# Hybrid decoder layer on one core: the four plain down-projection blocks row by row, a last half row in two 256-column pieces, 16 filler products instead of 24, and a new table of instruction places

## The chip, the cores and the metric

The kernel runs on one core of a Trainium2 chip. A time is the device time of one execution in microseconds (us). Before the change three runs took 617.90, 619.43 and 617.29 us, so the median is 617.9 us. A profiled execution has a time of its own and, a little shorter, a span: the time from its first to its last instruction. All positions in the trace are counted from the start of the span.

The engines are named as in the profile: PE is the matrix engine (PEld its weight loads), DVE the vector engine, ACT the scalar engine, POOL the general engine, and SP the engine that starts nearly all transfers.

## The reference: what is computed

One decoder layer for 512 tokens and a model width of 1024, in float32:

```
h = modulate(rms_norm(x, pre_norm_mix), sh1, sc1)
y = hybrid_mixer(h, ...)          # RG-LRU group and sparse-attention group, each RMS-normalised, then w_out
x = x + (1 + g1) * rms_norm(y, post_norm_mix)
h = modulate(rms_norm(x, pre_norm_mlp), sh2, sc2)
y = square(relu(h @ w_ff1)) @ w_ff2        # w_ff1: 1024 x 4096, w_ff2: 4096 x 1024
x = x + (1 + g2) * rms_norm(y, post_norm_mlp)
```

The six vectors sh, sc and g come from one product of silu(c) with a 1024 x 6144 matrix. The change is about the last product (the "down-projection" with w_ff2) and the last line, about the opening of the program, and about the order of everything between.

## The kernel before

**Precision.** Every large product is made from three products of a faster number format: an operand is split into a high part (hi, made by a copy on ACT or DVE) and a low part (lo, made by a subtraction on DVE or POOL), and `mm3` (line 908) multiplies hi by hi, hi by lo and lo by hi into the same PSUM bank. So each block of weights costs ACT, DVE and POOL work before PE may use it, and this splitting runs ahead of PE through four buffers of parts and four of raw weights (class `Weights`, line 469).

**Stages.** The opening loads x and the first weights, normalises x (`norm_x`), forms the first shift and scale by 16 narrow products with silu(c) (tile `tp`, from `sil` and `p` in the trace) and transposes x on PE. Before the transposes can start, PE runs filler products (`WARM`, lines 38 and 877): each multiplies a corner of x with the identity into a bank of the coming stage that is overwritten later; in the trace they are `s<-r,ident`, and one filler shows as two records. Then come the input projection ("first wave", matmuls `<-h,hi_a`), the recurrent group and the attention mixed with each other (roughly 50 to 260 us), the output projection, the up-projection with w_ff1 (280 to 450 us), and the down-projection (450 to 607 us).

**Down-projection.** w_ff2 has 32 blocks of 128 rows. 28 of them go through a scheme that saves products by adding blocks first: 14 pairs in a first pass (weights `D0` to `D13`), then a second pass (`e0` to `e13`). The last four blocks (28 to 31, weights `s28` to `s31`) are plain. Output is 4 rows of 128 tokens by 2 halves of 512 columns, eight half rows in eight PSUM banks; `rows` (lines 1774 and 1775) lists them. Before the change, block 28 is multiplied into all eight half rows first, and then the last `G_LAST` = 3 blocks half row by half row (line 1776). When a half row is done, DVE adds it to what the first pass left (`ob`), ACT squares it with a sum (`junk<-r`), and DVE or POOL multiply it by the row `g2row`; when both halves of a row are done, `finish` (line 1736) adds the two sums on DVE (`stat`), POOL takes the power -1/2 (`stat<-stat,nhalf`), DVE combines each half with x (SCALAR_TENSOR_TENSOR), and SP stores it (`out<-r`).

**Order.** The order written in the code isn't the order on the engines. Every operation is recorded as a node, and `flush` (line 274) issues the nodes in the order of a table of numbers, `PLAN`, one number per node; each engine then runs its own nodes in that order and waits where an input isn't there. `PLACE` says, for each operation that two or three engines could do, which one does it. Operations carry the line of a helper: 334 matmul, 337 transpose, 344 ACT, 376 DVE and POOL, 418 transfers started by SP.

## Time and profile before

| | before |
|---|---|
| three runs, us | 617.90, 619.43, 617.29 (median 617.9) |
| the profiled execution's time, us | 618.04 |
| its span, us | 616.3 |
| PE busy, share of the span | 590.4 us, 96% |
| DVE busy | 554.3 us, 90% |
| ACT busy | 406.1 us, 66% |
| POOL busy | 167.4 us, 27% |
| mean clock granted to PE | 0.993 |

PE is idle for 25.9 us of the span: until the first x has come, for some 12 us in short waits inside, and for 9 us at the end. A busy PE is not a PE at its peak: matmuls overlap, and a matmul's length in the trace includes its way through the array. The distance from one start to the next says more: it is about 0.227 us for 512 columns and 0.12 us for 256 columns in the dense stretches. Durations at one engine that follow each other overlap in the same way, by about 0.1 us.

### The profile page before, as it was taken

The numbers are of one execution on the slowest core, as the hardware profiler recorded it, in microseconds if no ns is written. First come the engines' busy times: TensorE is split into PE (matmuls) and PEld (weight loads), VectorE is DVE, ScalarE is ACT, GpSimd is POOL, SyncE is SP. The second block draws the span as 40 slices with busy tenths as digits, with TensorE's granted clock in tenths as the row PEclk, the third lists the DMA queues.
The fourth block names the chain that finished last, engine by engine and source line by source line (L and its number), as shares of the span: only waits on it lengthen the run. The fifth ranks groups of instructions, "written<-read, shape, count | busy, mean of one in ns | idle before, by whom it ended". The sixth has DMA issues, their size and how long they took to land.

```text
span 616.3 us, 10061 instructions
## 1 busy us (share of the span) xinstructions
PE 590.4 (96%) x3504; PEld 514.7 (84%) x3504; DVE 554.3 (90%) x1152; ACT 406.1 (66%) x824; POOL 167.4 (27%) x189
## 2 busy tenths in 40 slices
PE   6999999999889999999999999999998999999994
PEld 6888989977768898879999999998867888888883
DVE  5897999989989998889999989999899999999827
ACT  6546317999999899896856555656466666654312
POOL 5104010325335448541033233213000000211143
PEclk9999999999989999999999999999999999999998
DMA  8996994240305311022334323335423445443303
GB/s 350 369 351 264 336 367 171 102 151 22 129 11 204 137 36 35 0 87 69 137 137 138 110 97 121 104 103 188 137 87 115 149 130 163 162 138 109 130 0 137
DMA packets 26842, 89.10 MB, mean 145 GB/s; under 512 B 2980, under 2 KB 3236, under 8 KB 26792
## 3 DMA queue, kind: packets, MB, share of 16 engines
q1 hardware_dynamic: 26648, 88.40, 40.4%
q8 instruction: 27, 0.44, 0.3%
q14 instruction: 23, 0.19, 0.1%
q10 hardware_dynamic: 144, 0.07, 0.1%
HBM read 86.36 MB, written 2.10 MB: 144 GB/s over the span
## 4 chain that ended last, share of the span: by engine, by line
PE 76%; DVE 13%; ACT 7%; issue 2%; DMA 1%; POOL 0%; DVEq 0%; ACTq 0%
PE f L334 26%; PE s L334 18%; PE pv L334 16%; PE tp L334 12%; PE tp L337 4%; DVE fT L376 3%; DVE fl L376 1%; ACT p L344 1%; DVE lo_B L376 1%; DVE lo_C L376 1%; DVE lo_D L376 1%; ACT h L344 1%; ACT r L344 1%; ACT L344 1%; ACT junk L344 1%
## 5 line engine op out<-in xcount | busy, mean ns | idle before, releaser
L334 PE MATMUL f<-hi_o,h 128*128 128x512 f32 x128 | 46.1, 413 | 1.3 <-ACT h L344 1.1
L344 ACT ACTIVATE p<-p,mx 128x32 f32<-128x32 f32 (+4 forms) x96 | 45.1, 472 | 1.4 <-DVE mx L376 1.4
L344 ACT ACTIVATE hi_B<-raw_A 128x512 fp32r<-128x512 f32 x35 | 22.1, 631 | 28.5 <-DVE raw_A L376 21.0
L334 PE MATMUL pv<-pt,V 128*128 128x256 f32 x160 | 37.9, 308 | 2.3 <-ACT pt L344 2.1
L334 PE MATMUL s<-K,Q 128*128 128x288 f32 (+4 forms) x128 | 36.6, 333 | 0.8 <-DVE mx L376 0.8
L337 PE MATMUL tp<-ident,p 128*128 128x128 f32 x192 | 37.0, 273 | 0.4 <-DVE pt L376 0.4
L376 DVE TENSOR_TENSOR pt<-tp,pt 128x512 fp32r<-128x512 f32 (+1 forms) x56 | 33.9, 609 | 3.3 <-ACT pt L344 1.9
L344 ACT ACTIVATE fT<-fT 128x512 f32<-128x512 f32 x50 | 30.6, 623 | 2.7 <-DVE fT L376 2.2
L334 PEld LDWEIGHTS pv<-pt,V 128*128 128x128 f32 x160 | 27.0, 191 | 6.3 <-ACT pt L344 2.5
L376 POOL TENSOR_SCALAR p<-p,den 128x32 f32<-128x32 f32 (+4 forms) x33 | 28.9, 886 | 6.5 <-DVE den L376 2.9
L344 ACT ACTIVATE junk<-r 128x1024 bf16<-128x1024 f32 (+1 forms) x20 | 17.8, 888 | 16.8 <-DVE r L376 16.8
L337 PEld LDWEIGHTS tp<-ident,p 128*128 128x128 f32 x192 | 24.5, 140 | 4.8 <-issue 1.1
L376 DVE CUSTOM_DVE_ANT_0 p<-p,silb 128x1024 f32<-128x1024 f32 x23 | 27.9, 1221 | 0.1
L334 PEld LDWEIGHTS f<-hi_o,h 128*128 128x128 f32 x128 | 23.2, 189 | 5.4 <-ACT h L344 1.4
L334 PE MATMUL f<-lo_o,h 128*128 128x512 f32 x64 | 25.9, 410 | 0.0
L334 PEld LDWEIGHTS s<-K,Q 128*128 128x128 f32 x128 | 22.4, 188 | 3.4 <-issue 0.7
L344 ACT ACTIVATE hi_D<-raw_D 128x1024 fp32r<-128x1024 f32 x14 | 14.8, 1058 | 14.3 <-DVE raw_D L376 5.1
L334 PE MATMUL tp<-r,hi_B 128*128 128x256 f32 x96 | 23.0, 285 | 0.1
L344 ACT ACTIVATE pt<-tp 128x512 fp32r<-128x512 f32 (+1 forms) x38 | 19.8, 534 | 4.5 <-PE tp L337 3.5
L344 ACT ACTIVATE hi_e<-raw_e 128x1024 fp32r<-128x1024 f32 x13 | 13.8, 1062 | 13.5 <-PE s L334 4.3
L334 PE MATMUL pv<-r,hi_B 128*128 128x256 f32 x96 | 22.5, 284 | 0.0
L376 DVE TENSOR_TENSOR lo_B<-raw_A,hi_B 128x512 fp32r<-128x512 f32 x32 | 22.0, 686 | 0.5 <-ACT hi_B L344 0.2
(424 smaller groups left out, 2312.0 us busy)
## 6 DMA issues: line engine op xcount, KB each, us to landing
p<-in_ada_a SPq DMA_DIRECT2D x16, 512.0 KB, 7.4
ar<-in_ada_r SPq DMA_DIRECT2D x16, 512.0 KB, 4.1
p<-in_ada_t SPq DMA_DIRECT2D x16, 512.0 KB, 5.5
raw_d<-in_wd SPq DMA_DIRECT2D x14, 512.0 KB, 3.2
raw_e<-in_wd SPq DMA_DIRECT2D x14, 512.0 KB, 3.4
raw_A<-in_wf SPq DMA_DIRECT2D x12, 512.0 KB, 3.3
raw_B<-in_wf SPq DMA_DIRECT2D x12, 512.0 KB, 3.7
r<-in_x SPq DMA_DIRECT2D x8, 512.0 KB, 4.7
```

Of the source, the lines that this page charges most:

```text
L334: lambda: self.nc.tensor.matmul(out, lhs, rhs, start=start, stop=stop))
L337: self.issue("pe", 0.109, [out], [src], lambda: self.nc.tensor.transpose(out, src, ident))
L344: return "act", cost, lambda: self.nc.scalar.activation(out, src, func, scale=scale, bias=bias, **kw), func
L376: return eng, cost, lambda: fn(out, *args, **kw), None
```

## The change

`WARM` goes from 24 to 16. `G_LAST` goes from 3 to 4: no block is multiplied into all half rows first any more, and all four plain blocks are taken half row by half row. The last half row in the list (row 3, columns 0 to 511) is no longer accumulated on top of the second pass: that pass's bank is closed and added to `ob` early, and the four blocks go into two fresh banks as two pieces of 256 columns, each with its own sum of squares; `finish` for that row adds three sums instead of two and stores three parts instead of two. `PLAN` and `PLACE` are new tables throughout.

```diff
-G_LAST = 3
+G_LAST = 4
-WARM = 24
+WARM = 16
 PLAN = (
-    '###(#8#A#&#M#E#1#5#7#;#C#T#Y#`#b#k#=#B#P#p#z#$#%#)#-#+#,#.#2#J#/#w#[#0#6#9#D#I#h#l#n#t#|#~$$$-$2$4$8'
...
 def times(what, way, fs, w, first, last, ts=(0, 1)):
-            mm3(into[what, t], [p[:, c0 + t * P:c0 + t * P + P] for p in fs[e]], ws, first, last)
+            mm3(into[what, t], [p[:, c0 + t * P:c0 + t * P + P] for p in fs[e]], ws, first, last and (what != 4 or t > 0))
-    def square(t, n):
-        o = ob[t][:, half(n)]
-        act(junk[:, half(n)], o, AF.Square, scale=D ** -0.5, accum_out=ssq[t][:, n:n + 1])
-        either("tensor_mul", o, o, g2row[n])
+    def square(t, n, c=slice(0, 512), k=None):
+        o, k = ob[t][:, half(n)][:, c], n if k is None else k
+        act(junk[:, half(n)][:, c], o, AF.Square, scale=D ** -0.5, accum_out=ssq[t][:, k:k + 1])
+        either("tensor_mul", o, o, g2row[n][:, c])
-    def finish(t):
+    def finish(t, last=False):
         o, ss = ob[t], ssq[t]
-        dve("tensor_scalar", ss[:, 0:1], ss[:, 0:1], ss[:, 1:2], EPS, op0=ALU.add, op1=ALU.add)
+        if last:
+            dve("tensor_scalar", ss[:, 0:1], ss[:, 0:1], ss[:, 2:3], None, op0=ALU.add)
+        else:
+            dve("tensor_scalar", ss[:, 0:1], ss[:, 0:1], ss[:, 1:2], EPS, op0=ALU.add, op1=ALU.add)
         pool("tensor_tensor", ss[:, 0:1], ss[:, 0:1], nhalf[:, 0:1], op=ALU.pow)
-        for n in (t > 1, t < 2):
-            dve("scalar_tensor_tensor", o[:, half(n)], o[:, half(n)], ss[:, 0:1], late["x2"][t][:, half(n)],
-                op0=ALU.mult, op1=ALU.add)
-            load(out[tok(t), half(n)], o[:, half(n)])
+        parts = [half(t > 1), half(t < 2)]
+        if last:
+            parts[1:] = [slice(0, 256), slice(256, 512)]
+        for sl in parts:
+            dve("scalar_tensor_tensor", o[:, sl], o[:, sl], ss[:, 0:1], late["x2"][t][:, sl], op0=ALU.mult, op1=ALU.add)
+            load(out[tok(t), sl], o[:, sl])
...
-            for row, n, ps in rows:
+            for row, n, ps in rows if group is not plain[1] else rows[:-1]:
...
+            if group is plain[1]:
+                row, n, ps = rows[-1]
+                dve("tensor_add", ob[row][:, half(n)], ps, ob[row][:, half(n)])
+                for k in range(2):
+                    c, ps = slice(256 * k, 256 * k + 256), bank("s" if k else "pv")[:, :256]
+                    for f in group:
+                        yield lambda: 0.0
+                        mm3(ps, [z[:, tok(row)] for z in fs[f]], [z[:, half(n)][:, c] for z in W.get(f"s{f}")],
+                            f == 2 * NJ, f == NF - 1)
+                    o = ob[row][:, half(n)][:, c]
+                    dve("tensor_add", o, ps, o)
+                    square(row, n, c, 2 * k)
...
+                finish(row, True)
```

The new tables move instructions on all engines. Three places matter for what follows.

PE at the opening, from after the products for `silb` to the first matmul of the input projection. `s_154<-r_1_87,ident` is a filler, `tp_166<-sil` a product for the first shift and scale, `tp_169<-ident,r` a transpose of x. The last rows before:

```order
L337 MATMUL tp_169<-ident,r_2_88 128x128
L334 MATMUL s_154<-r_1_87,ident 128x128 x2
L334 MATMUL tp_166<-sil,p_157 128x1
L334 MATMUL s_154<-r_1_87,ident 128x128
L334 MATMUL tp_166<-sil,p_157 128x1 x2
L337 MATMUL tp_169<-ident,r_2_88 128x128
L334 MATMUL tp_166<-sil,p_158 128x1 x4
L334 MATMUL s_154<-r_1_87,ident 128x128 x6
L334 MATMUL s_154<-h_135,hi_a_173 128x512
```

And now:

```order
L334 MATMUL s_154<-r_1_87,ident 128x128
L334 MATMUL tp_166<-sil,p_158 128x1
L337 MATMUL tp_169<-ident,r_1_87 128x128
L334 MATMUL tp_166<-sil,p_158 128x1 x2
L337 MATMUL tp_169<-ident,r_1_87 128x128
L337 MATMUL tp_169<-ident,r_2_88 128x128 x2
L334 MATMUL s_154<-r_1_87,ident 128x128 x4
L334 MATMUL f_152<-h_135,hi_a_173 128x512
```

Before, 18 of 24 fillers stood ahead of the last of the 16 products `tp_166` and six behind it; now 12 stand ahead of it and four behind. The transposes, which were spread among fillers, now stand together at the end.

ACT in the attention stage, where the functions that ACT holds in a table change between exp (`p_...,sm<-p,mx`) and the gelu of the recurrent group's gate branch (`r_205_421<-r_205_421`). Before:

```order
L344 ACT_TABLE_LOAD
L344 ACTIVATE r_205_421<-r_205_421 128x512
L344 ACT_TABLE_LOAD
L344 ACTIVATE p_459,sm_458<-p_459,mx_457 128x128 x2
L344 ACTIVATE hi_o_447<-raw_o_335 128x1024
L344 ACTIVATE pt_479<-tp_478 128x512
```

And now:

```order
L344 ACTIVATE pt_479<-tp_478 128x512
L344 ACTIVATE r_205_421<-f_435 128x512
L344 ACTIVATE hi_o_447<-raw_o_335 128x1024
L344 ACTIVATE p_461,sm_458<-p_461,mx_457 128x32
L344 ACTIVATE p_461,sm_458<-p_461,mx_457 128x128 x2
L344 ACT_TABLE_LOAD
L344 ACTIVATE r_205_421<-r_205_421 128x512
```

One gelu that stood alone between two table loads now waits for its neighbour; the program has 10 table loads instead of 12, and both that are gone were here. The copy `pt_479`, which stood behind the two loads, now stands ahead of the next one.

DVE at the end. `f_1266` is the bank of row 3, columns 512 to 1023, `tp_1264` (before) that of row 3, columns 0 to 511, `pv_1400` and `s_1401` (now) the two pieces that take its place. The last rows before:

```order
L376 TENSOR_TENSOR r_640_1116<-f_1266,r_640_1116 128x512
L376 TENSOR_TENSOR r_640_1116<-tp_1264,r_640_1116 128x512
L376 SCALAR_TENSOR_TENSOR r_640_1116<-r_640_1116,stat,r_369_606 128x512
L376 TENSOR_SCALAR stat<-stat 128x1
L376 SCALAR_TENSOR_TENSOR r_640_1116<-r_640_1116,stat,r_369_606 128x512
L376 TENSOR_TENSOR r_640_1116<-r_640_1116,g2row_758 128x512
L376 SCALAR_TENSOR_TENSOR r_640_1116<-r_640_1116,stat,r_369_606 128x512
L376 TENSOR_TENSOR r_640_1116<-r_640_1116,g2row_757 128x512
L376 SCALAR_TENSOR_TENSOR r_640_1116<-r_640_1116,stat,r_369_606 128x512
```

And now:

```order
L376 TENSOR_TENSOR r_640_1116<-pv_1400,r_640_1116 128x256
L376 TENSOR_TENSOR r_640_1116<-s_1401,r_640_1116 128x256
L376 SCALAR_TENSOR_TENSOR r_640_1116<-r_640_1116,stat,r_369_606 128x512
L376 TENSOR_TENSOR r_640_1116<-f_1266,r_640_1116 128x512
L376 SCALAR_TENSOR_TENSOR r_640_1116<-r_640_1116,stat,r_369_606 128x512
L376 TENSOR_SCALAR stat<-stat 128x1 x2
L376 TENSOR_TENSOR r_640_1116<-r_640_1116,g2row_758 128x512
L376 SCALAR_TENSOR_TENSOR r_640_1116<-r_640_1116,stat,r_369_606 128x512
L376 TENSOR_TENSOR r_640_1116<-r_640_1116,g2row_757 128x256
L376 SCALAR_TENSOR_TENSOR r_640_1116<-r_640_1116,stat,r_369_606 128x256 x2
```

Before, the two last half rows of row 3 ended together and were added one behind the other. Now both pieces are added ahead of `f_1266`, which still ends last and is still 512 columns wide; on PE the last five rows are all `f_1266`.

More of the change, by code (lines that the diff above doesn't have):

```diff
@@ L165 @@
[L165 to L169 removed]
+    '###(#*#s#&#@#J#4#7#9#:#G#=#A#F#K#P#D#N#g#q#t#$#%#,#.#)#-#/#3#?#0#z#L#2#8#;#Q#T#X#d#j#n#r#|$5$E$I$K$M'
@@ L177 @@
           'dddaddadddaddadddaddadddaddadddaddadddaddadddaddadddaddadddaddadddaddadddaddadddaddadddaddadadda'
[L178 to L183 removed]
+          'dadpadaddadaddadaddadaddadaddadaddadaddadaddadaddadaddddaddddaddadaddpapad',
@@ L184 @@
+         'AW': 'aaddaadappppdpdd',
+         'AS': 'paaapdapdaaddadpaapdddpaapaapdpdpddpppdaapdppaaapdaaadaappdddadppappaddpappapdppapappdpappppapda'
+          'apppaapaadppapda',
+         'AV': 'aaaaaddaaddaaddaadaaaaaaaaadaaaaadaaaaaaadaadaaaaaaadaaa',
+         'VW': 'dpppppdpddddpdddppd',
          'AD': 'dd',
-         'FA': 'pppppdppppdp',
-         'RS': 'ppapdaddaddd',
-         'TH': 'ddpdaaddddddaadpadpdaadpadpdaadddaddaddaddaddddd',
+         'FA': 'ppppppppppdp',
+         'RS': 'ppappaddaddd',
@@ L1771, in down_all @@
                     nxt = second_pair(j + 1) if j + 1 < NJ else one(2 * NJ)
-                times(what, SECOND_WAY, fs, w, j == 0, False)
+                times(what, SECOND_WAY, fs, w, j == 0, what == 4 and j == NJ - 1)
             W.drop(f"e{j}")
@@ L1791, in down_all @@
                         finish(row)
+            if group is plain[1]:
[10 more added lines that the diff above has]
+                    square(row, n, c, 2 * k)
+                    if k == 0:
+                        dve("tensor_scalar", ssq[row][:, 0:1], ssq[row][:, 0:1], ssq[row][:, 1:2], EPS, op0=ALU.add,
+                            op1=ALU.add)
+                finish(row, True)
             for f in group:
```

241 lines of the change are left out of this document (118 added, 123 removed).

## The prediction

> **What bounds the kernel now.** I read the page first: busy shares, then the chain that ended last.
>
> ```profile
> PE 590.4 (96%) x3504; PEld 514.7 (84%) x3504; DVE 554.3 (90%) x1152; ACT 406.1 (66%) x824; POOL 167.4 (27%) x189
> PE 76%; DVE 13%; ACT 7%; issue 2%; DMA 1%; POOL 0%; DVEq 0%; ACTq 0%
> ```
>
> PE is the limit in the large: three quarters of the chain run through it. So a gain can only come from less work on PE, from its waits, or from the ends of the span where it does nothing useful. The list of waits says where PE stood; these are the four longest of 15 rows, which add up to 16.4 us.
>
> ```profile
> PE s L334 <- DMA r<-in_x: 4.7, 1, 4.7
> PE pv L334 <- ACT pt L344: 2.4, 2, 2.1
> PE f L334 <- DVE lo_D L376: 2.0, 2, 1.5
> PE f L334 <- ACT h L344: 1.1, 1, 1.1
> ```
>
> Without the 4.7 us for the first x, 11.7 us of waits lie inside; the rest of PE's 25.9 idle us is the end. Last, the busy time by stretch, whose columns are the stretch, its length, then PE, PEld, DVE, ACT and POOL busy, the granted clock, and the transfers:
>
> ```profile
> 160.00:172.00 12.00, 9.55 (x49) 7.58 (x48) 11.30 (x31) 11.62 (x29) 6.28 (x8) 0.92 0.48 168
> 380.00:400.00 20.00, 20.00 (x164) 19.68 (x163) 18.99 (x36) 11.41 (x20) 6.60 (x6) 1.00 0.32 106
> 445.00:476.00 31.00, 28.39 (x119) 21.46 (x118) 30.62 (x53) 19.78 (x35) 1.00 (x1) 1.00 0.28 94
> 476.00:606.00 130.00, 130.00 (x575) 107.34 (x574) 115.18 (x180) 69.96 (x113) 19.61 (x11) 1.00 0.38 122
> ```
>
> The reader is to see two things. From 160 to 172 us ACT (11.62 of 12) and DVE (11.30) are full while PE is not: there the order on ACT sets the pace. From 445 to 476 us DVE is full (30.62 of 31) and PE waits. From 476 us to the end of the products PE never waits.
>
> **The end.** This is the part that the change rewrites by hand. First PE's last product, then what follows it on DVE, ACT and POOL:
>
> ```profile
> 606.90 0.39 PE L334 MATMUL f<-hi_s,fl 128*128 128x512 f32 x1
> 607.33 0.69 DVE L376 TENSOR_TENSOR r<-f,r 128x512 f32<-128x512 f32 x1
> 608.11 0.63 ACT L344 ACTIVATE junk<-r 128x512 bf16<-128x512 f32 x1 [2.18 <-DVE r L376]
> 609.26 0.19 ACT L344 ACTIVATION_READ_ACCUMULATOR junk<-r 128x1 f32 x1
> 609.48 0.21 DVE L376 TENSOR_SCALAR stat<-stat 128x1 f32<-128x1 f32 x1
> 609.77 0.99 POOL L376 TENSOR_TENSOR stat<-stat,nhalf 128x1 f32<-128x1 f32 x1 [0.90 <-DVE stat L376]
> 611.06 0.75 DVE L376 SCALAR_TENSOR_TENSOR r<-r,stat,r 128x512 f32<-128x512 f32 x1
> 611.73 0.69 DVE L376 TENSOR_TENSOR r<-r,g2row 128x512 f32<-128x512 f32 x1
> 612.45 0.75 DVE L376 SCALAR_TENSOR_TENSOR r<-r,stat,r 128x512 f32<-128x512 f32 x1
> L376 DVE TENSOR_TENSOR fl<-fS,fh 128x256 fp32r<-128x256 f32 x36 | 15.0, 418 | 0.0
> ```
>
> PE ends at 606.90 + 0.39 = 607.29, DVE at 612.45 + 0.75 = 613.20: 5.91 us, and 3.1 us more until the store has landed and the span ends at 616.3. In the new order both pieces of the other half row are added ahead of `f`, so one square of 512 columns is left behind the last add instead of two. With this row's own steps: add at +0.04; its square from +0.82 to +1.55 (0.63 and the read of the sum, 0.19, overlapping 0.1); the two sums one behind the other, 0.2 each, until +2.0; the power until +3.05; DVE takes it up 0.3 later, as here (610.76 to 611.06), at +3.35; then the 512-column combination (0.65 to the next start), a 256-column multiply and two 256-column combinations (0.42 each by the last row, 0.35 to the next start): +3.35 + 0.65 + 3 x 0.35 = +5.05. That is 0.85 us less than 5.91. Its last store is half as large; I give that nothing. Ends: 0.4 us of gain if the pieces' squares are in ACT's way, 1.3 us if DVE does the 256-column multiply while the power runs. The price of the pieces: 24 products of 256 columns (20.00 us for 164, 0.122 us each, in the stretch at 380 us) for 12 of 512 (0.227 us from start to start here): 2.93 - 2.72 = **+0.2 us**.
>
> **The plain blocks.** Before, 24 products of block 28 (24 x 0.227 = 5.4 us) covered the splitting of blocks 29 to 31. That cover is gone from the code, but the new table mixes half rows, so I counted products in the order. The slowest splitter is POOL:
>
> ```profile
> L376 POOL TENSOR_TENSOR lo_s<-raw_s,hi_s 128x1024 fp32r<-128x1024 f32 x3 | 8.1, 2703 | 13.9 <-DVE hi_s L376 13.9
> 586.24 1.06 ACT L344 ACTIVATE hi_s<-raw_s 128x1024 fp32r<-128x1024 f32 x1 [5.51 <-PE pv L334]
> ```
>
> POOL makes the low parts of blocks 29 and 30, one behind the other: 2 x 2.7 us, or 6.6 us at 3.3 each. Their buffers come free with the last products of `e12`, and from there to the first use of block 30's low part lie 43 products, 9.8 us; a cast of 0.7 us and 6.6 us fit. The added wait is DVE's add of the closed bank, right behind the second pass's last product into it; the low part of block 31 and the first half rows' adds queue behind it, and PE needs that low part only some 38 products (8.6 us) later. I cost this at nothing; if the cover fails, the price is one low part on POOL, up to 3.3 us. A gain is excluded: PE did not wait here before.
>
> **The opening.**
>
> ```profile
> 4.75 1.62 PE L334 MATMUL s<-r,ident 128*128 128x128 f32 x6 [4.75 <-DMA r<-in_x]
> 7.87 2.16 PE L334 MATMUL tp<-ident,sil 128*128 128x128 f32 x10
> 14.12 0.61 PE L334 MATMUL s<-r,ident 128*128 128x128 f32 x4
> 14.57 0.27 PE L337 MATMUL tp<-ident,r 128*128 128x128 f32 x1
> 14.16 0.29 DVE L376 TENSOR_SCALAR r<-r,stat 128x128 f32<-128x128 f32 x1 [2.92 <-POOL stat L376]
> 16.08 0.95 PE L334 MATMUL tp<-sil,p 128*128 128x1 f32 x8
> 17.07 0.22 DVE L376 SCALAR_TENSOR_TENSOR sa<-tp,ab,vecs 128x1 f32<-128x1 f32 x1 [1.75 <-PE tp L334]
> 17.45 1.02 ACT L344 ACTIVATE h<-tp,sa 128x256 fp32r<-128x256 f32 x2 [1.99 <-DVE sp L376]
> 18.52 0.50 PE L334 MATMUL s<-h,hi_a 128*128 128x512 f32 x1
> ```
>
> PE is busy without a gap from 4.75 to 18.5 us, yet DVE waits 1.75 us for its sums, and ACT 1.99 us behind DVE: the fillers are in the way. x was scaled at 14.16 + 0.29 = 14.45 us, and its transpose came at 15.9. Two fillers (four records) take 14.57 - 14.12 = 0.45 us, 0.225 each; six fewer stand ahead of the last sum: 6 x 0.225 = 1.35 us, so the first real product could come at 17.2 us. The next things in line are the last scaling of x at about 14.5 us and the high part of the first weights, both earlier. But the new order also gives DVE two more casts and one more low part of these first weights, which POOL and ACT did before, and DVE is nearly as full as PE in the first wave. I take two thirds: **-0.9 us**, ends 0 and 8 x 0.225 = 1.8. One transfer of ada weights goes ahead of the third x tile on SP's queue; that tile is due at PE four us later than it arrives.
>
> **The table loads.** ACT and PE before:
>
> ```profile
> 164.42 1.28 ACT L344 ACT_TABLE_LOAD   x1
> 165.71 0.63 ACT L344 ACTIVATE r<-r 128x512 f32<-128x512 f32 x1
> 166.36 1.28 ACT L344 ACT_TABLE_LOAD   x1
> 169.51 0.60 ACT L344 ACTIVATE pt<-tp 128x512 fp32r<-128x512 f32 x1
> 170.16 0.58 PE L334 MATMUL pv<-pt,V 128*128 128x256 f32 x1 [2.11 <-ACT pt L344]
> 178.48 0.50 PE L334 MATMUL f<-hi_o,h 128*128 128x512 f32 x1 [1.06 <-ACT h L344]
> ```
>
> The copy `pt` for which PE waited 2.11 us stood behind two loads and the gelu between them; both loads are gone, 2 x 1.28 = 2.57 us on an engine that is full here. The second wait, 1.06 us, stays: a load and a gelu still precede `h`. If DVE (11.30 of 12) is the next limit, little is left. Ends 0 and 2.6; nearer to the wait that ended with `pt`: **-1.5 us**. The Trainium skill (ScalarE: Activation LUTs, What ACT_TABLE_LOAD costs) puts a switch of tables at 2.66 us, a load of 1.28 and a drain of 1.38. The rows agree on the load and show no drain: the gelu starts at 165.71, 0.01 us after the load. By the page the two loads would be worth 5.3 us on ACT.
>
> **All other waits.** The tables reorder every engine, so the remaining waits, 11.7 - 2.1 = 9.6 us, are drawn anew. I see no reason for a sign; the first pass of the down-projection shows the size (2.6 us of PE's 31). I take 0, ends -4 and +4.
>
> **The sum** against the profiled execution, 618.04 us (span 616.3): -0.85 + 0.2 + 0 - 0.9 - 1.5 + 0 = -3.05, so 615.0. That execution lies 0.14 us above the median of the runs, so **614.9 us**.
>
> **The rivals.** (1) *Hidden anyway.* The first wave and the attention run at DVE's pace, and what starts earlier waits there: only the end is left, 618.04 - 0.85 + 0.2 - 0.14 = 617.2. For it: DVE at 11.30 of 12 at 160 us; against it: PE's wait there ended with ACT. (2) *More.* The waits on `lo_D` and what surrounds them go as well:
>
> ```profile
> 473.07 0.50 PE L334 MATMUL f<-lo_D,fh 128*128 128x512 f32 x1 [1.52 <-DVE lo_D L376]
> ```
>
> PE's 31 us there hold 2.6 us of waits: 614.9 - 2.6 = 612.3. For it: seven more other products now stand ahead of that one on PE; against it: DVE has no room. (3) *Slower: DVE late in the first pass.* The low part of the second half of `D1` moves in DVE's order from ahead of its sister to far behind it. Each time DVE falls behind by a low part (1.2 us) and an addition (0.7), PE waits 1.9 us. It decides from the third such wait on: 614.9 + 3 x 1.9 = 620.6. For it: 30.62 of 31; against it: PE waited only twice for DVE there. (4) *The clock.* Fewer fillers leave PE slow for longer: until 9.87 us a 128-column product took 0.43 us (five in 2.16 us from 7.87), later 0.225. If that came back ahead of the first wave, another five us at half speed would cost 2.5 us: 617.4. The granted clock of the opening shows no drop after 9.87. The Trainium skill (TensorE: Matmul & The Clock Gate, Part 1) has such a gate close after an idle window of about 3.4 us; by it nothing happens here, as the pause behind four fillers stays under one us.
>
> **How the numbers follow.** Forecast 0.44, (1) 0.24, (2) 0.17, (3) 0.10, (4) 0.05. The forecast's own range is 613.3 to 616.0. 0.3% is 1.85 us, about what a measurement here can tell from no change: under 616.05 is faster, over 619.75 slower. Faster: 0.44 + 0.17 = 0.61; no change 0.24 + 0.05 = 0.29; slower 0.10. The range leaves out (3) and the lower part of (2): 612.0 to 618.2.
>
> **What would show it.** End: DVE's last instruction 5.0 to 5.2 us after PE's last product. Opening: the first `hi_a` product near 17.2 us. Tables: ten loads, and no wait of PE on `pt` over 1 us between 155 and 180 us. Plain blocks: no wait of PE on `lo_s`. The forecast is wrong if the first wave or attention ends no earlier than before, or if PE's inner waits add up to over 14 us.

## The result and the profile after

The changed kernel takes 611.95 us (median of 6 runs, 611.55 to 612.39), beside it the kernel before 617.6 (616.01 to 619.8). The ratio is 0.9906 [0.9883, 0.9929]: 5.7 us faster, 0.9%, where 3.0 were forecast. On another chip the same pair gave 611.80 (611.44 to 612.28) and 617.87 (615.75 to 620.39), ratio 0.9897 [0.9873, 0.9922]. Besides being faster, the new kernel spreads less from run to run: 0.8 us instead of almost 4. The old kernel's spread goes with the clock granted to PE: of 46 of its executions on two chips, 15 took 615.79 to 616.45 us at a mean clock of 0.995 or 0.996 and the others 617.15 us or more, all but one at 0.991 to 0.993, so that against the first group alone the gain would be some 4.2 us (an estimate across chips).

The profiled execution took 612.0 us with a span of 610.2 (before 618.04 and 616.3). Its busy times and the shares of the chain by engine:

```profile
PE 588.3 (96%) x3500; PEld 511.5 (84%) x3500; DVE 560.2 (92%) x1160; ACT 405.7 (66%) x827; POOL 163.3 (27%) x183
PE 79%; DVE 12%; ACT 6%; issue 1%; DMA 1%; POOL 0%; POOLq 0%; DVEq 0%; ACTq 0%
```

The same work, with PE's share of the chain up by 3 points. The five longest waits of PE (us in total, times, longest):

```profile
PE s L334 <- DMA r<-in_x: 4.7, 1, 4.7
PE pv L334 <- DVE pt L376: 2.0, 2, 1.7
PE s L334 <- DVE mx L376: 1.3, 2, 0.9
PE tp L334 <- DVE g2row L376: 1.0, 1, 1.0
PE pv L334 <- ACT hi_D L344: 1.0, 1, 1.0
```

All rows add up to 13.1 us (16.4 before), so the waits inside are 8.4 us instead of 11.7: 3.3 of the 6.1 us. Where the 6.1 us of span lie shows a comparison of the two PE rows at equal progress: each product of one trace is set beside the product at which the other PE had done the same amount of product work, and their starts are subtracted (new minus before, us).

| PE at about | 20 | 140 to 157 | 177 to 181 | 196 to 245 | 337 | 370 | 417 | 527 to 585 | last product |
|---|---|---|---|---|---|---|---|---|---|
| new minus before | -1.2 | +0.2 to -1.2 | -1.5 to -3.4 | -2.2 | -2.0 | -4.8 | -5.3 | -5.4 | -5.2 |

Where a range stands, the two orders do different products, and the comparison can be read to about a microsecond only. Four things are to be seen. The opening gains 1.2 us, of which at most a part is left at 140 us. By 196 us 2.2 are won in all. Between 337 and 417 us, in the up-projection, 3.3 us more are won, of which my prediction says nothing. And the end behind the last product gives the rest, 0.9.

The opening: fillers and the first product of the input projection.

```profile
15.98 1.06 PE L334 MATMUL s<-r,ident 128*128 128x128 f32 x8
17.25 0.50 PE L334 MATMUL f<-h,hi_a 128*128 128x512 f32 x1 [0.22 <-ACT h L344]
```

That product starts at 17.25 us instead of 18.52. The stretches that the prediction showed, in the same columns (PE, PEld, DVE, ACT, POOL busy, clock, transfers):

```profile
160.00:172.00 12.00, 9.96 (x52) 7.82 (x52) 11.55 (x31) 10.22 (x34) 7.67 (x8) 1.00 0.54 182
380.00:400.00 20.00, 20.00 (x167) 19.76 (x166) 19.15 (x38) 11.82 (x21) 6.13 (x7) 1.00 0.38 120
445.00:476.00 31.00, 28.98 (x125) 22.87 (x124) 30.62 (x52) 19.61 (x33) 1.11 (x1) 1.00 0.37 119
```

ACT has fallen from 11.62 to 10.22 of 12 us in the attention stage and DVE is now the full one; the clock there is 1.00 instead of 0.92. In the first pass of the down-projection DVE is as full as before (30.62 of 31) and PE waits 2.0 us instead of 2.6. The end of the new kernel:

```profile
601.69 0.39 PE L334 MATMUL f<-hi_s,fl 128*128 128x512 f32 x1
602.12 0.69 DVE L376 TENSOR_TENSOR r<-f,r 128x512 f32<-128x512 f32 x1
604.14 0.93 POOL L376 TENSOR_TENSOR stat<-stat,nhalf 128x1 f32<-128x1 f32 x1 [1.49 <-DVE stat L376]
605.10 0.75 DVE L376 SCALAR_TENSOR_TENSOR r<-r,stat,r 128x512 f32<-128x512 f32 x1 [0.44 <-POOL stat L376]
606.11 0.88 DVE L376 SCALAR_TENSOR_TENSOR r<-r,stat,r 128x256 f32<-128x256 f32 x2
```

From the end of the last product, 601.69 + 0.39 = 602.08, to DVE's end at 606.99 pass 4.91 us, where it was 5.91.

### The profile page after: what moved, and what is told of

Same layout as the page of the kernel before. It is cut to its first block, busy times and chain, and to the rows that moved or that the text cites. A ratio compares the mean times of both kernels' runs of the same rounds, so it can differ in the third digit from the quotient of the medians.

```text
span 610.2 us, 10061 instructions
## 1 busy us (share of the span) xinstructions
PE 588.3 (96%) x3500; PEld 511.5 (84%) x3500; DVE 560.2 (92%) x1160; ACT 405.7 (66%) x827; POOL 163.3 (27%) x183
## 4 chain that ended last, share of the span: by engine, by line
PE 79%; DVE 12%; ACT 6%; issue 1%; DMA 1%; POOL 0%; POOLq 0%; DVEq 0%; ACTq 0%
PE f L334 25%; PE s L334 19%; PE pv L334 18%; PE tp L334 14%; PE tp L337 4%; DVE r L376 2%; DVE p L376 2%; DVE fT L376 1%; ACT r L344 1%; ACT p L344 1%; DVE lo_C L376 1%; ACT L344 1%; DVE fl L376 1%; ACT junk L344 1%; ACT h L344 1%
## 5 line engine op out<-in xcount | busy, mean ns | idle before, releaser
L344 ACT ACTIVATE hi_B<-raw_A 128x512 fp32r<-128x512 f32 x33 | 20.7, 629 | 30.7 <-DVE raw_A L376 22.3
L334 PE MATMUL s<-K,Q 128*128 128x288 f32 (+4 forms) x128 | 34.8, 335 | 1.4 <-DVE mx L376 1.3
L376 POOL TENSOR_SCALAR p<-p,den 128x32 f32<-128x32 f32 (+4 forms) x36 | 30.4, 855 | 12.0 <-DVE den L376 7.4
L344 ACT ACTIVATE hi_D<-raw_d 128x1024 fp32r<-128x1024 f32 x14 | 14.8, 1060 | 22.0 <-DVE raw_d L376 11.4
L344 ACT ACTIVATE junk<-r 128x1024 bf16<-128x1024 f32 (+2 forms) x21 | 17.9, 851 | 16.1 <-DVE r L376 16.0
L344 ACT ACTIVATE pt<-tp 128x512 fp32r<-128x512 f32 (+1 forms) x44 | 23.2, 533 | 3.6 <-PE tp L337 2.4
L376 POOL TENSOR_TENSOR fl<-fT,fh 128x512 fp32r<-128x512 f32 x2 | 4.1, 2064 | 78.0 <-ACT fh L344 70.6
L334 PE MATMUL f<-third,hi_B 128*128 128x256 f32 x96 | 23.4, 284 | 0.0
```

What stands on the lines that cost most here:

```text
L334: lambda: self.nc.tensor.matmul(out, lhs, rhs, start=start, stop=stop))
L344: return "act", cost, lambda: self.nc.scalar.activation(out, src, func, scale=scale, bias=bias, **kw), func
L376: return eng, cost, lambda: fn(out, *args, **kw), None
```

## The experiments

The theory at the start was the prediction's own: the end, the opening and the table loads each give what they are worth alone. The rival: most of the gain is the redrawn waits, which I had set to 0. For this parts of the new order were put into the old kernel and parts of the old order into the new one. Such a kernel has the same instructions on both sides of the cut; only their order changes there. The joint can add a wait of its own, which is named where the trace shows one. What a kernel takes "over the new kernel" is counted from 611.80 us throughout, on whatever chip it ran; the new kernel itself differed by 0.15 us between two chips. A diff line for `PLAN` stands for its numbers.

**One part alone: the opening.** The old kernel, with 16 fillers and the new order up to the first products of the input projection.

```diff
-WARM = 24
+WARM = 16
 PLAN = (
-  # the old numbers as far as the first products of the input projection
+  # the new numbers as far as there, and the old behind them
...
```

> The old code with 16 fillers; the new order up to the first six products of the input projection (rank 145 of 5431 common operations, about 18 us), the old order for all that follows. Reading of the two traces: the first product of the input projection comes at 17.2 us instead of 18.5, and the 1.2 us are kept to the end: 1.0 to 1.3 us less than before. By the prediction's term: 0.9 less. Rival 'hidden anyway': the first wave waits elsewhere, 0.0 to 0.3 less.

618.69 us (617.1 to 622.57), beside it 618.3: ratio 1.0018 [1.0, 1.0037]. In its trace PE starts the first wave early and then waits there for `lo_a` and `r` from DVE (0.21 and 0.28 us) and for `h` from ACT (0.43), all between 18 and 24 us; by 36 us a lead of 0.47 is a lag of 0.23. Alone on the old order the opening is worth nothing.

**The new order up to the end of the attention.**

```diff
-WARM = 24
+WARM = 16
 PLAN = (
-  # the old numbers
+  # the new numbers up to rank 2349 (about 247 us), and the old behind them
...
```

> 16 fillers, the new order up to the end of the attention (rank 2349, about 247 us, where both orders have done exactly the same operations), then the old order. Reading of the two traces: 2.0 us less than before (opening 1.2, attention 0.8), and the granted clock at full in the stretch of 160 to 182 us. By the prediction's terms (opening 0.9, table loads 1.5): 2.4 less. Rival: the attention runs at the pace of DVE, only what the opening gives, 1.2.

617.31 (615.94 to 618.5): 0.9986 [0.9972, 1.0]. So opening, input projection, gates and attention of the new order together give 1.0 us on the old kernel, and the interval just reaches no change. In its profiled execution the granted clock is full from 160 to 182 us, but 0.50 from 16 to 18 us, in the opening.

**All but the tail.** As above, with the cut at rank 5227 (about 575 us); the last pass and its code are the old ones.

```diff
-  # the new numbers up to rank 2349
+  # the new numbers up to rank 5227 (about 575 us), and the old behind them
...
```

> 16 fillers, the new order up to the last pairs of the second pass of the down-projection (rank 5227, about 575 us), then the old order and the old code of the last blocks. Reading of the two traces: 5.2 us less than before, that is 3 us more than the order up to the attention alone. By the prediction's terms nothing is added after the attention: 2.4 less.

613.71 (613.49 to 614.1): 0.9929 [0.9916, 0.9943]. Beyond the attention another 3.6 us come. The joint costs something (PE waits 0.47 us for `lo_e` at 570.5), and the end lasts 5.91 us from the last product to DVE's last instruction, as before.

**The tail alone.** The new tail, with its pieces and its code, behind the old order.

```diff
-G_LAST = 3
+G_LAST = 4
 PLAN = (
-  # the old numbers of the last pass
+  # the new numbers of the last pass
...
```

> The new code of the last blocks and its order from the last pairs of the second pass on; 24 fillers and the old order up to there. By the prediction (end 0.85, pieces -0.2): 0.65 us less. Reading of the two traces: from the last product to the last DVE instruction 4.9 us instead of 5.9, with 0.2 for the pieces: 0.8 less. A rival in which the plain blocks lose their cover: a wait of PE on the low parts of blocks 29 to 31, up to 3.3 us more instead.

619.27 (616.93 to 621.32): 1.0011 [0.9996, 1.0026]. The end lasts 4.90 us, which is as short as in the new kernel, and still the time doesn't fall: the joint holds a wait of 0.45 us, and this execution shows two longer waits in the first pass of the down-projection, which was not touched (1.11 and 1.22 us, where before had 0.58 and 0.48). Against a kernel whose runs spread over 4 us, a tail of 0.9 can't be told from nothing.

What the four say: up to the attention 1.0, from there to the tail 3.6, the tail 0.9 by its trace. The rival holds. The next three take parts *out* of the new kernel.

**New kernel, old opening.** 24 fillers and the old order as far as the first products.

```diff
-WARM = 16
+WARM = 24
 PLAN = (
-  # the new numbers as far as the first products of the input projection
+  # the old numbers as far as there, and the new behind them
...
```

> The new kernel with 24 fillers and the old order up to the first products of the input projection (rank 145); everything behind is new. By the prediction's term the new opening is worth 0.9: 0.9 more than the new kernel (611.95). By its start alone, 18.5 us instead of 17.25: 1.2 more. Theory now, from the progress of PE in both traces (1.2 us ahead at 20 us, 0.3 us ahead at 140 us): the first wave and the early attention give the lead back; 0 to 0.3 more.

614.01 (612.64 to 618.48): 0.9949 [0.9932, 0.9966], 2.2 us over the new kernel. The execution with the profile is the longest of the twelve, 618.48 us; the next took 615.51. It lost about 1.24 us in the opening, and then this, with a stretch behind it:

```profile
67.99 1.80 PE L334 MATMUL s<-r,raw_c 128*128 128x64 f32 x8 [1.55 <-DMA raw_c<-in_wc]
```

```profile
68.00:70.00 2.00, 2.00 (x9) 2.00 (x10) 1.97 (x4) 1.22 (x2) 0.00 (x0) 0.55 1.08 332
```

PE waits 1.55 us for a transfer, and then the granted clock is half for some 7 us (0.50 from 70 to 74 us). The whole lag grows to 6.3 us by 80 us. This isn't where the 2.2 us of the median come from: the other eleven executions have a mean clock of 0.995 to 0.998, this one 0.990. In this profile the opening gives 1.2 us; what makes up the rest of the 2.2 stays open.

**New kernel, old order from 125 to 192 us.** This takes the attention stage back, with its two table loads.

```diff
 PLAN = (
-  # the new numbers at ranks 1225 to 1790
+  # the old numbers there
...
```

> The new kernel with the old order from rank 1225 to 1790 of the common operations (about 125 to 192 us), which brings back the lone gelu between two table loads. Theory now: the wait of 2.1 us on the copy pt comes back, and behind it PE runs at about half its clock for 3.6 us, as in the profile before: 1.8 us more than the new kernel, of which the waits are a few tenths only and the clock 1.6. By the prediction's term (table loads 1.5 without any clock): 1.5 more, with the clock at full. Rival: DVE sets the pace there, 0 to 0.3 more.

613.21 (612.4 to 614.32): 0.9935 [0.9918, 0.9953], 1.4 us over the new kernel. PE again waits for `pt` from ACT, and the clock falls behind that wait:

```profile
169.47 0.39 PE L334 MATMUL pv<-pt,V 128*128 128x256 f32 x1 [2.13 <-ACT pt L344]
```

```profile
170.00:172.00 2.00, 2.00 (x6) 1.53 (x6) 1.44 (x3) 1.98 (x9) 0.56 (x2) 0.54 0.00 0
```

**New kernel, old order in the up-projection** (289 to 419 us).

```diff
 PLAN = (
-  # the new numbers at ranks 2751 to 4139
+  # the old numbers there
...
```

> The new kernel with the old order from rank 2751 to 4139 (about 289 to 419 us, the up-projection). By the prediction nothing changes there: 0. By the lists of waits (1.9 us of gaps before, 0.7 after): 1.2 more than the new kernel. By the distances from start to start (excess over the even pace 6.5 us before, 3.4 after): 3.1 more.

615.95 (615.35 to 616.21): 0.9976 [0.9963, 0.9988], 4.1 us over the new kernel. This is the largest part, and it lies where I had seen no reason for a sign. The trace of before shows what happens there: three instructions on POOL and DVE, and PE's waits.

```profile
336.99 1.30 POOL L376 TENSOR_TENSOR lo_B<-raw_A,hi_B 128x512 fp32r<-128x512 f32 x1 [0.16 <-ACT hi_B L344]
337.04 1.79 DVE L376 TENSOR_TENSOR lo_C<-raw_B,hi_C 128x512 fp32r<-128x512 f32 x1
338.61 0.28 PE L334 MATMUL f<-h2l,hi_B 128*128 128x256 f32 x1
339.69 0.39 PE L334 MATMUL pv<-s4h,hi_C 128*128 128x256 f32 x1 [0.80 <-DVE fT L376]
359.68 1.73 POOL L376 TENSOR_TENSOR lo_C<-raw_A,hi_C 128x512 fp32r<-128x512 f32 x1
360.18 1.78 DVE L376 TENSOR_TENSOR lo_C<-raw_B,hi_C 128x512 fp32r<-128x512 f32 x1
362.01 0.38 PE L334 MATMUL pv<-s4h,lo_C 128*128 128x256 f32 x1 [0.78 <-DVE lo_C L376]
```

Two subtractions of 128x512, one on POOL and one on DVE, run at the same time, and DVE's lasts 1.79 us; with POOL elsewhere the same subtraction takes 0.68 (below). PE then waits for DVE. The new table gives these two of POOL's subtractions to DVE.

**The same, with two low parts on DVE.** The kernel of the run above; two of POOL's subtractions move to DVE as in the new table, and nothing else.

```diff
 DVE:
 TENSOR_TENSOR fT_846<-pv_931,fT_846 128x256
+TENSOR_TENSOR lo_B_938<-raw_A_911,hi_B_937 128x512
...
 TENSOR_TENSOR fT_849<-s_967,fT_849 128x256
+TENSOR_TENSOR lo_C_976<-raw_A_945,hi_C_975 128x512
 POOL:
-TENSOR_TENSOR lo_B_938<-raw_A_911,hi_B_937 128x512
...
-TENSOR_TENSOR lo_C_976<-raw_A_945,hi_C_975 128x512
```

> The new kernel with the old order of the up-projection (which measured 615.95), but two low parts that the old table gives to POOL (starts 336.99 and 359.68 us in the profile before) given to DVE, as in the new table. Theory: they blocked the low parts on DVE that took 1.79 and 1.78 us instead of 0.68, and these made PE wait at 339.69 and 362.01; each wait cost PE 1.06 us from start to start. Both gone: 2.1 less, 613.8; both halved, since DVE has 0.6 us more to do: 1.0 less. Rival: the 4 us come from other places of that stretch: no change, 616.

614.99 (614.87 to 615.47): 0.9954 [0.9935, 0.9974], 1.0 us less than without the move. The two kernels ran on different chips, and the highest run here (615.47) lies just above the lowest there (615.35). First DVE in the run above, then here:

```profile
335.22 1.79 DVE L376 TENSOR_TENSOR lo_C<-raw_B,hi_C 128x512 fp32r<-128x512 f32 x1
```

```profile
335.25 0.68 DVE L376 TENSOR_TENSOR lo_C<-raw_B,hi_C 128x512 fp32r<-128x512 f32 x1
336.18 0.68 DVE L376 TENSOR_TENSOR lo_B<-raw_A,hi_B 128x512 fp32r<-128x512 f32 x1
```

One instruction more on DVE, and DVE is done earlier: 0.68 + 0.68 is less than 1.79. PE's two waits of 0.79 and 0.77 us go, and 0.16 and 0.37 stand there instead. So this cause is shown for 1.0 of the 4.1 us. Much of the rest lies at the same two places: at equal progress, the kernel with the old up-projection falls behind the new one by 1.2 us from 334 to 342 us and by 1.6 from 350 to 370, and by about 1 us in all the rest of the stage. The move wins back 0.6 and 0.7 there, since DVE has one subtraction more to do each time. What else the new order does at these places is not assigned to single instructions; more such meetings of POOL and DVE stand at about 396, 411 and 421 us in that kernel, but no run took them away one by one.

**Can the same be done in the attention?** In the new kernel DVE's scan meets a low part on POOL, and PE waits for the `pt` behind it:

```profile
164.48 2.40 POOL L376 TENSOR_TENSOR lo_o<-raw_o,hi_o 128x1024 fp32r<-128x1024 f32 x1
164.73 3.23 DVE L376 TENSOR_TENSOR_SCAN r<-p,r 128x512 f32<-128x512 f32 x1
168.98 0.68 DVE L376 TENSOR_TENSOR pt<-tp,pt 128x512 fp32r<-128x512 f32 x1
169.71 0.51 PE L334 MATMUL pv<-pt,V 128*128 128x256 f32 x2 [1.69 <-DVE pt L376]
```

First try: that low part goes to DVE, behind the scan, and another one to POOL.

```diff
 DVE:
+TENSOR_TENSOR lo_o_428<-raw_o_332,hi_o_427 128x1024
 TENSOR_TENSOR r_124_337<-r_124_337,r_205_421 128x512
...
-TENSOR_TENSOR lo_o_475<-raw_o_420,hi_o_474 128x1024
 POOL:
-TENSOR_TENSOR lo_o_428<-raw_o_332,hi_o_427 128x1024
 TENSOR_SCALAR p_444<-p_444,den_446 128x32
+TENSOR_TENSOR lo_o_475<-raw_o_420,hi_o_474 128x1024
```

> The new kernel with one low part of the output weights moved from POOL (164.48 to 166.88 us, beside a scan on DVE that takes 3.23 us instead of 1.2) to DVE behind the scan, and another one from DVE (173.53, 1.22 us) to POOL, which is idle then. Theory: the scan was held up by POOL's subtraction; it takes 1.2 to 1.4 us, the wait of 1.69 us of PE at 168.0 goes, 1.5 to 1.9 us less than the new kernel at that place. If DVE sets the pace until 180 us, part of it comes back as a wait there: 0.5 less at least. Rival: the scan is long by itself, then it stays at 3.2 us and nothing changes.

614.02 (612.68 to 614.32): 0.9944 [0.9925, 0.9963], 2.2 us slower than the new kernel.

```profile
165.18 1.22 DVE L376 TENSOR_TENSOR_SCAN r<-p,r 128x512 f32<-128x512 f32 x1
171.56 2.52 POOL L376 TENSOR_TENSOR lo_o<-raw_o,hi_o 128x1024 fp32r<-128x1024 f32 x1 [6.26 <-ACT hi_o L344]
171.78 2.85 DVE L376 TENSOR_TENSOR r<-r,r 128x512 f32<-128x512 f32 x1
175.44 0.79 PE L334 MATMUL f<-hi_o,h 128*128 128x512 f32 x1 [2.58 <-ACT h L344]
```

The scan falls from 3.23 to 1.22 us, as that theory says. But the subtraction now on POOL meets DVE's next instruction, which takes 2.85 us (0.69 in the new kernel), and PE waits 2.58 us, behind which the granted clock is 0.50 from 176 to 178 us: the meeting was moved, not removed.

Second try: the scan itself goes behind the addition of `pt`.

```diff
 DVE:
-SCALAR_TENSOR_TENSOR r_124_337<-p_417,r_201_414 128x512
...
 TENSOR_TENSOR pt_480<-tp_478,pt_479 128x512
+SCALAR_TENSOR_TENSOR r_124_337<-p_417,r_201_414 128x512
```

> The new kernel with one instruction of DVE moved: the scan that took 3.23 us beside POOL's subtraction (164.48 to 166.88 us) is put behind the addition pt for which PE waits 1.69 us; what comes forward reads one operand from the banks of products. Theory: a DVE instruction with two operands in the on-chip memory does not run while POOL's subtraction does, one that reads a bank of products does. Then the addition ends at 166 instead of 169.6 us, PE's wait at 168.0 goes, the scan ends as before: 1.5 to 1.9 us less than the new kernel. Rival: DVE is the limit until 180 us, the wait comes back there: 0 to 0.5 less.

> The new kernel unchanged, on the chip of this comparison, as the measure for the three others: 611.6 to 612.4 as before. Its runs lie close together where those of the old kernel spread over 4 us.

611.23 (610.82 to 611.65), ratio 0.9888 [0.9861, 0.9915]; the new kernel beside it 611.80 (611.44 to 612.28). The ranges still touch. The profile is of the shortest execution, 610.82 us; beside the new kernel's first profile, PE is 1.4 us ahead in it from 176 us to the end. It is the best version that ran.

```profile
164.29 2.40 POOL L376 TENSOR_TENSOR lo_o<-raw_o,hi_o 128x1024 fp32r<-128x1024 f32 x1
165.56 0.29 DVE L376 CUSTOM_DVE_ANT_0 p<-s,tab 128x128 f32<-128x128 f32 x1 [1.03 <-PE tp L337]
166.60 0.68 DVE L376 TENSOR_TENSOR pt<-tp,pt 128x512 fp32r<-128x512 f32 x1
167.20 1.22 DVE L376 TENSOR_TENSOR_SCAN r<-p,r 128x512 f32<-128x512 f32 x1
```

Here DVE's two instructions that start beside the same subtraction on POOL read a product bank (`s`, `tp`), and they keep their 0.29 and 0.68 us; the scan starts after POOL and takes 1.22.

**More waits of DVE's.** On top of the later scan, `g2row` three rows earlier on DVE; and then, in another kernel, also six instructions that nothing waits for put behind the first pass's low parts, and one cast earlier on ACT.

```diff
 DVE:
 TENSOR_TENSOR lo_D_1102<-raw_D_1086,hi_D_1101 128x1024
+SCALAR_TENSOR_TENSOR g2row_758<-tp_1110,g2row_758 128x512
...
-SCALAR_TENSOR_TENSOR g2row_758<-tp_1110,g2row_758 128x512
```

> As the scan behind the addition, and besides the multiplication that frees the bank for which PE waits 1.02 us at 451.25 (start to start 1.3 us too long) three DVE instructions earlier, right behind the low part of D1. Theory: 0.9 less than without it, 2.4 to 2.8 less than the new kernel in all, if nothing else is late by then: 609.3. Rival: DVE is full in this stretch, so PE waits for the next low part instead: no change beside the scan alone.

> As the scan behind the addition, and at the start of the first pass of the down-projection six DVE instructions whose result PE needs 14 us later or more are put behind those that it needs at once, the multiplication that frees the bank comes forward by three, and the high part of D1 on ACT by two. Theory: PE's waits of 0.99 us (hi_D) and 1.04 us (g2row) at 447 to 452 us shrink by half or more, and the postponed instructions find room before 466 us: 0.8 to 1.5 less than with the scan alone (611.2). Rival, as with g2row alone: DVE is full until 476 us, the wait comes back on a low part: 0.

611.63 (611.27 to 612.09) and 611.31 (611.09 to 611.56), ratios 0.9894 and 0.9908 [0.9891, 0.9925]: neither is faster than the later scan alone. In the first the wait of 1.0 us for `g2row` is gone from PE's list and one for `lo_D`, not in the list of the scan kernel, has come:

```profile
PE f L334 <- DVE lo_D L376: 0.6, 1, 0.6
```

DVE is full in that stretch; what is taken earlier pushes something else back.

**The table loads or the place of the copy?** In the old kernel the copy `pt` goes ahead of the gelu and its two loads, which stay.

```diff
 ACT:
+ACTIVATE pt_479<-tp_478 128x512
 ACT_TABLE_LOAD
 ACTIVATE r_205_421<-r_205_421 128x512
 ACT_TABLE_LOAD
...
-ACTIVATE pt_479<-tp_478 128x512
```

> The old kernel with one instruction of ACT moved: the copy pt, for which PE waits 2.11 us at 168.0, is made ahead of the gelu and its two table loads (its transposes are done at 164.0); both loads stay. Theory: the wait goes, and with it the half clock from 170 to 173.6 us, 1.6 us; some of it comes back as other waits up to 190 us, as with the old order of this stretch in the new kernel (2.1 at 176 us, 0.9 at 190 us). 1 to 2 us less than before, and a smaller spread of the runs. By the prediction's term the loads cost 1.5 us by their length on ACT: no change as long as they stay.

618.04 (617.18 to 618.98), 1.0012 [1.0002, 1.0023]: no gain. PE now waits 1.38 us for an `h` at 168.2 and three times more behind it (0.71, 0.64, 1.03), and the clock falls later instead (the stretches of this kernel):

```profile
178.00:180.00 2.00, 1.68 (x6) 1.40 (x7) 2.00 (x4) 1.68 (x4) 0.00 (x0) 0.84 0.04 8
180.00:184.00 4.00, 4.00 (x13) 2.51 (x12) 2.93 (x8) 3.84 (x12) 1.09 (x1) 0.65 0.01 2
```

By then I had a theory that the wait for `pt` and the clock behind it were the whole price. The run doesn't settle it: as long as the loads stay, other waits and another stretch at half clock come in place of those removed. This would fit the prediction's term, by which the loads have to be paid somewhere in the stage; but of the four waits three end with DVE and one with ACT, so that ACT's length is the price is argued and not shown.

**The new order up to the end of the first wave, on the old kernel** (about 45 us).

```diff
-WARM = 24
+WARM = 16
 PLAN = (
-  # the old numbers up to rank 410
+  # the new numbers there
...
```

> The old code with 16 fillers, the new order up to rank 410 (about 45 us: opening and most of the input projection), then the old order. Theory: the lead of 1.2 us that the new opening gives was lost with the old order behind it because DVE and ACT were late in the first wave there (waits of 0.20, 0.27 and 0.42 us between 18 and 24 us); with the new order of the first wave 0.8 to 1.2 us of it are kept: 617.0. Rival: the old order needs what its own opening had prepared on DVE, and the lead is lost at the next joint: 617.9.

617.13 (615.92 to 618.53), 1.0002 [0.9989, 1.0016]: no gain that could be measured, as with the opening alone.

**What does a wait of 2 us cost?** New kernel, with the addition of `pt` one instruction later on DVE.

```diff
 DVE:
-TENSOR_TENSOR pt_480<-tp_478,pt_479 128x512
 ISA p_499,mx_497<-s_500,tab 128x384
 ISA mx_497 128x1
+TENSOR_TENSOR pt_480<-tp_478,pt_479 128x512
```

> The new kernel with the addition pt, for which PE waits 1.69 us at 168.0 without any loss of clock, one DVE instruction (0.55 us) later: the wait is 2.24 us. If a wait of over 2 us by itself halves the clock for 3.4 us, as in the old kernel (2.11 us), PE is 2.1 us late at 176 us, and 1 to 2 us are left at the end. If the clock depends on where a wait falls, the granted clock stays at 1.00 in some or all runs: 0.5 us late, 0 to 0.5 left at the end.

614.03 us as the median of 612.24, 612.84, 614.0, 614.06, 614.36 and 614.47; 0.9946 [0.9929, 0.9962]. The execution with the profile is the one of 612.24. There PE waits 2.15 us, nothing is lost later, and the clock stays full there:

```profile
168.00:170.00 2.00, 0.00 (x0) 0.00 (x0) 2.00 (x13) 1.41 (x7) 0.00 (x0) 1.00 0.92 340
170.00:172.00 2.00, 2.00 (x11) 1.78 (x12) 1.93 (x6) 1.99 (x3) 0.00 (x0) 1.00 1.01 241
```

Four other runs of the same kernel take some 2 us longer. Whether the clock fell behind the wait in those stays open. Their mean clocks, 0.993 and 0.994, are no lower than those of the two short runs, both 0.993; but the profiled one has a stretch at half clock in the opening (0.50 from 16 to 18 us) and loses next to nothing by it, so the means don't tell.

**The fillers alone.** New kernel, eight fillers added back, nothing else.

```diff
-WARM = 16
+WARM = 24
```

> The new kernel with eight more fillers, six of them ahead of the last of the 16 products for the first shift and scale, two behind it; nothing else moves. By the prediction's rows (0.225 us each): the first product of the input projection 1.35 to 1.6 us later than 17.25 us. By the prediction's term two thirds of it at the end: 0.9 more than the new kernel (611.8). Since the lead of the new opening stayed to the end in the run with the old opening: 1.2 to 1.6 more. Rival: hidden in the first wave, 0.

615.93 (614.46 to 616.58): 0.9961 [0.9946, 0.9976], 4.1 us over the new kernel. First the opening's rows, then a stretch of it:

```profile
17.54 2.77 PE L334 MATMUL s<-r,ident 128*128 128x128 f32 x12
19.96 0.61 PE L334 MATMUL f<-h,hi_a 128*128 128x512 f32 x1
```

```profile
18.00:20.00 2.00, 2.00 (x12) 2.00 (x11) 1.47 (x3) 1.87 (x4) 0.00 (x0) 0.50 1.04 414
```

The first product comes 2.7 us later, and not the 1.35 to 1.8 that the fillers' number gives: PE runs the last of them at half clock, though it has been busy without a gap since 4.7 us. The number of fillers alone doesn't decide that: the profile of the old kernel, with 24, has no such stretch, and that of the unchanged new kernel on the other chip, with 16 and 612.27 us, has one:

```profile
16.00:18.00 2.00, 2.00 (x9) 1.61 (x8) 2.00 (x5) 1.87 (x4) 0.00 (x0) 0.54 1.09 371
```

Both new kernels have the half clock here, so a comparison of these two profiles leaves it out: with 24 fillers PE is 2.0 us behind at 25 us, near the 1.8 of eight fillers at 0.225, and still 2.0 at 65 us. Then comes a wait of 1.11 us for the same `raw_c`, until 68.6 us, and from there on the lag is 3.4 us. Why this transfer comes too late for PE, no run shows.

**The last half row whole.** New kernel, but its code is the old one apart from the four plain blocks and 16 fillers: no pieces, the new order.

```diff
-  # the new tail with its 256-column pieces
+  # the old tail: the last half row in whole 512-column products
 G_LAST = 4
 WARM = 16
```

> The new kernel with the last half row (row 3, columns 0 to 511) as 512 columns again, accumulated on the bank of the second pass, all four plain blocks half row by half row as before; every other instruction keeps its place. The half row's products stand where those of the first piece stood, its addition where that of the second piece stood, so the 512 columns that end last are the same. By the prediction: the end 0.85 longer without its smaller pieces if that is where the 0.85 come from, 0.2 less for 12 products of 512 columns instead of 24 of 256: 0.65 more. Theory now: the gain at the end comes from the order (one half row added ahead of the last product) and not from the pieces; then 0.2 us less on PE stand against one 512-column multiplication and one combination in place of 256 columns (0.3 us each more on DVE, after the power): 0.2 to 0.4 more at the end of DVE, 0 to 0.2 more in time.

612.03 (611.86 to 612.2): 0.9902 [0.9882, 0.9922]. Its last product and its DVE's last instruction:

```profile
601.08 0.39 PE L334 MATMUL f<-hi_s,fl 128*128 128x512 f32 x1
605.77 0.75 DVE L376 SCALAR_TENSOR_TENSOR r<-r,stat,r 128x512 f32<-128x512 f32 x1
```

From 601.47 to 606.52 are 5.05 us, 0.14 more than with the pieces, and the last product ends 0.6 earlier. Both kernels take the same time within their spread: the pieces give nothing that can be measured. The 0.9 us at the end come from the order, which adds the other half row ahead of the last product.

## Why the prediction was right and wrong

The direction was right and so was the mechanism at the end; the size was half of it, 3.0 us forecast and 5.7 measured, and most of the rest came from where nothing was forecast. The time lies 0.05 us below the low end of the range.

- **The end, -0.85.** Right: 5.05 us were predicted behind the last product, 4.91 measured, 1.0 less than before. The reason given was half right: the order does it, not the pieces, whose own price of +0.2 us can't be seen either.
- **The plain blocks, 0.** Right: PE has no wait behind 452.3 us.
- **The opening, -0.9.** The first product is where it was put (17.2 predicted, 17.25 measured), so "0.225 each" held. What this is worth at the end was mis-sized, in both directions: nothing on the old order, where the first wave gives it back, as rival (1) says; 2.2 us in the new kernel with the old opening and 4.1 with only the fillers back. The step that failed here is "two thirds": behind the new order the first wave took nothing of the eight fillers' 2.0 us, and 1.4 more came with the transfer of `raw_c`, of which the term knows nothing.
- **The table loads, -1.5.** The size came out, since undoing the stage costs 1.4 us, but by luck: the mechanism was another. The wait for `pt` that the term was to remove is mostly still there: the sign set for it did not come, for PE still waits over 1 us, 1.69 after 2.11, now behind DVE's scan of 3.23 us. What went is the half clock that followed the wait of before, and that the prediction had not priced. The rows of before and then of the new kernel, same columns as above:

```profile
170.00:172.00 2.00, 1.84 (x5) 1.58 (x6) 1.64 (x5) 1.73 (x6) 1.25 (x3) 0.53 0.02 6
172.00:174.00 2.00, 2.00 (x8) 1.64 (x7) 0.94 (x2) 1.10 (x7) 0.20 (x1) 0.61 0.00 0
```

```profile
170.00:172.00 2.00, 2.00 (x13) 1.75 (x13) 1.93 (x8) 1.99 (x3) 0.00 (x0) 1.00 1.06 301
```

- **All other waits, 0.** This is the step that made the number wrong: "I see no reason for a sign". The up-projection alone gives 4.1 us by the undo, and 3.3 by the comparison at equal progress; 1.0 of it is shown to be POOL beside DVE, and the cause of the rest stays open. A reason was to be seen in the trace of before: DVE's subtraction of one size and form lasted 1.79 us in two places and 0.68 in others, and PE waited behind both of the long ones, while the new order moves the two subtractions of POOL's beside them to DVE. I had read the list of waits by their sum and by the longest, and not asked of the middle ones why their releaser was late.
- **The rivals.** (1) holds for the opening on the old order, not for the whole. (2), at 612.3, comes near the time but by another way: the waits of the down-projection's first pass fell only from 2.6 to 2.0 us. (3) did not come. (4) did not come in the new kernel's first profile. On the other chip the same kernel's profile has half clock in the opening (16 to 19.6 us), and PE is only 0.4 us behind the first profile at 35 us, not 2.5. Of the two signs set for being wrong neither came: by 245 us 2.2 us are won, and PE's inner waits add up to 8.4 us.

The parts don't add up. Undone in the new kernel they cost 2.2, 1.4, 4.1 and, for the tail, 1.9 us (613.71 against 611.80), some 9.6 in all for a gain of about 6; alone on the old kernel the same opening and tail give nothing. Joints add waits, and a lag in one stage can be swallowed or made larger in the next. How much of the 9.6 is the joints stays open.

## What to carry to other kernels

Before setting the waits of a re-ordered kernel to zero, group the instructions of one form and look for those that last two or three times as long as their like: here they were DVE's, beside POOL, with PE waiting behind them, and moving the neighbour onto the "fuller" engine made it faster. Price a part within the kernel that it will run in, not alone on the old one, and look for the granted clock right behind each wait and in the opening, in more than one execution.

## What the runs showed of the hardware

**DVE beside POOL.** In the rows above, a DVE instruction with two operands in on-chip memory that starts beside an operation of POOL's ends a fixed time after POOL does, as if it waited for POOL and then ran: a TENSOR_TENSOR of 128x512 ends 0.54 to 0.55 us behind POOL's end (alone it takes 0.68), and the scan 1.08 us behind it (alone 1.22). So it lasts 1.79 us instead of 0.68, 2.85 instead of 0.69, and the scan 3.23 instead of 1.22. It goes the other way round too: POOL's subtraction at 359.68 us in the trace of before starts beside one of DVE's (359.58, 0.68 us) and takes 1.73 us instead of 1.30. DVE instructions that read a product bank (the rows of the later scan) kept their 0.29 and 0.68 us beside POOL's subtraction. The Trainium skill (GPSIMD Engine Reference, 1. Specifications) says that POOL shares its ways into the on-chip memory with VectorE, and names instructions of two such operands; the rows agree, and the sizes are theirs.

**The granted clock.** It fell to half behind waits of PE of 2.11 us (before), 2.13 us (old attention), 2.58 us (swapped low parts) and 1.55 us (old opening), and stayed at 1.00 behind 1.69 us (new kernel) and 2.15 us (`pt` later). The kernel with the new order up to the first wave has both outcomes, against the length of the waits: the clock is 1.00 from 170 to 174 us, behind the first of these rows, and 0.50 from 452 to 454 us, behind the second.

```profile
169.51 0.39 PE L334 MATMUL pv<-pt,V 128*128 128x256 f32 x1 [2.12 <-ACT pt L344]
451.45 0.80 PE L334 MATMUL f<-lo_D,fh 128*128 128x512 f32 x1 [1.21 <-DVE lo_D L376]
```

It also fell without any gap, to 0.54 at 16 to 18 us (new kernel on the other chip) and to 0.50 at 18 to 20 us (24 fillers), while PE ran transposes, fillers and the first products. In the rows of before, 170 to 174 us hold 3.4 us at half clock (a mean of 0.53 over 2 us is 1.88 us at half, one of 0.61 is 1.56); with the old opening it was 6.8. The Trainium skill (TensorE: Matmul & The Clock Gate, Part 1) speaks of a free-running window of some 3.4 us, and of the place of the first product in it for when the clock rises. That the place of a wait in such a window decides whether the clock falls is an inference from this; the length of the falls and waits of like length with both outcomes agree with it. That a whole idle window is needed, as the same section of the Trainium skill has it, doesn't agree: none of these waits is as long. What in the opening brings the fall, and why in some executions only, no run here shows.

**A stall costs more than its wait.** In the old up-projection PE's product at 338.61 and the next at 339.69 are 1.08 us apart, where the list of waits has 0.80; products of this size follow each other in 0.12 us otherwise. So that stall cost 0.96. So a sum of waits can understate what removing them gives, which is one more part of why 3.3 us of waits fewer came with more than that in time.
